# Modulation vectors summed over the partitions: column-of-ones matmuls, or a fold on VectorE ahead of four small matmuls

## The chip, the cores and the metric

One core of one Trainium2 chip runs the whole program. The metric is the device time of one execution in microseconds (us). Three runs of the kernel before took 1532.04, 1532.3 and 1536.19 us; their median is 1532.3 us. Engines are named as in the profile: PE (TensorE), DVE (VectorE), ACT (ScalarE), POOL (GpSimd) and SP, which issues the loads.

## What is computed

The reference is one step of a trunk of two layers for 384 tokens (128 of context, 256 latent) with 1024 features, all in float32. Each layer is a SwiGLU block, an attention mixer and a second SwiGLU block. Every one of these sub-layers takes a shift, a scale and a gate per feature, for two groups of tokens. These come from one linear map per layer:

```
def _adaln(cvec, w, b):
    m = jax.nn.silu(cvec) @ w + b
    return m.reshape(cvec.shape[0], N_MOD, D_MODEL)     # N_MOD = 9, D_MODEL = 1024

h = _rms_norm(x, g[0]) * (1 + m[:, :, 1]) + m[:, :, 0]
x = x + 0.5 * m[:, :, 2] * _swiglu(h, w13[0], w2[0])
```

So a layer has nine vectors m of 1024 features, each for two conditioning vectors (context and latent). The change concerns how these vectors are added up.

## The kernel before, in words

Activations lie feature-major: eight chunks of 128 features by 384 tokens. Each float32 operand of a large product is split into a high and a low part, and a product is three matmuls (`mm3`, L176 to L180): high by high (L178), high by low (L179), low by high (L180). Weights come as tiles of 1024 rows by 256 columns through a stream (`Weights`). SP loads three tiles ahead (L75), ACT makes the high half `wh` (L80) and DVE the low half `wl` (L84), again three tiles ahead of their use.

A SwiGLU block (`ffn`, `swiglu`) goes through the hidden features in three stages. Each stage first makes its chunks of gates and ups: products named proj, silu on ACT to `sg` (L611), `gf` as their product on DVE (L618), then the split of `gf` into `gh` on ACT (L628) and `gl` on DVE (L629). Then come eight products named down, which read all `gh` and `gl` of the stage, and DVE adds each to the residual `x` (L359). Products go to four PSUM buffers in turn.

The first two modulation vectors are made apart, chunk by chunk, in the setup. The other 16 are made beside the large products. A weight chunk `wm` of 128 rows by 1024 columns is loaded for each of eight k. In `tick`, the first chunk's product with the two conditioning columns is written by ACT to two accumulators `macc` of 128x1024 (L217, L218), and the other seven are added by DVE, one multiply-add for each accumulator (L221). For the first of the 16 vectors a part of that goes over ACT (L226) and POOL (L227), and DVE does one accumulator (L228). `pace` is called after each chunk of a product and decides by a rate whether a tick is issued. When the last k of a vector is done, `m_sums` is set and no tick is issued for three further calls (`mod_finish`, called after each chunk). Then `mod_sum` issues the sum over the 128 partitions. Eight matmuls at L269, four for each accumulator, have a column of ones as weights and 256 of the 1024 columns as the moving operand; each goes to its own 32 partitions of a PSUM tile `m_sum`. In the trace a float32 matmul shows as two passes, so a vector has sixteen. DVE then transposes blocks of 32x32 (L274, `m_tr`), and `mod_place` adds the bias (L288) and finishes scales (L290) and halved gates (L295). The ticks that were held back follow at once.

All engines run their instructions in the order in which the program issues them, and the order is the one written here. Setup fills `onecol` by memsets on POOL (L1331, L1333).

Of the kernel before, what the change touches and what calls it, by code (L numbers as in the profile page):

```python
# [8 lines left out]
F32 = mybir.dt.float32  # L9
# [3 lines left out]
ALU = mybir.AluOpType  # L13
AX = mybir.AxisListType

P = 128
D = 1024
# [41 lines left out]
class Weights:  # L59
    """A stream of weight tiles: loads run ahead, then each is split into two float32r parts."""  # L60
# [37 lines left out]
    def start_half(self):  # L98
        """The high parts of the next half tile."""
        if self.cur is None:  # L100
            self.load(self.ns + 1)
            self.cur = (self.raw.pop(self.ns), self.split_tiles())
            self.at = 0
        self.end = min(self.at + 4, self.units[self.ns].nk)
        self.high(*self.cur, self.at, self.end)

    def end_half(self):
        """The low parts of it."""
        k = self.k
        self.low(*self.cur, self.at, self.end, k.nc.gpsimd if self.at and k.light else k.nc.vector)  # L110
        self.at, self.end = self.end, 0
        if self.at == self.units[self.ns].nk:
            self.parts[self.ns] = self.cur[1]
            self.cur = None
            self.ns += 1
            self.load(self.ns + self.LOADED)
# [7 lines left out]
    def refill_half(self):  # L124
        """A half tile at a time, the low parts a call after the high ones."""
        if self.end:
            self.end_half()
        if self.ns < min(self.np + self.SPLIT, len(self.units)):
            self.start_half()
# [16 lines left out]
class Unit:  # L146
    """A weight tile: nk row chunks of 128 from r0, 256 columns from c0."""
# [6 lines left out]
class Kernel:  # L154
# [20 lines left out]
    def mm3(self, out, w, x, first, last):  # L175
        """out += w.T @ x over float32 operands given as (high, low) float32r parts."""  # L176
        mm = self.nc.tensor.matmul
        mm(out, w[0], x[0], start=first, stop=False)  # L178
        mm(out, w[0], x[1], start=False, stop=False)  # L179
        mm(out, w[1], x[0], start=False, stop=last)  # L180
# [5 lines left out]
    def rsqrt_cols(self, v, out):  # L186
        """out = v ** -0.5 for a few columns."""
        n = v.shape[-1]
        self.nc.gpsimd.tensor_tensor(out=out, in0=v, in1=self.neghalf[:, 0:n], op=ALU.pow)  # L189

# [11 lines left out]
    def tick(self, n=1):  # L202
        """n row chunks of the next modulation vectors: products and sums over the rows of a partition."""
        nc = self.nc
        self.m_debt += n
        while self.m_debt:
# [26 lines left out]
            if k == KC - 1:  # L233
                self.m_sums, self.m_wait = (l, i), 3

    def pace(self):
        """A chance for ticks: as many as the rate of this part has added up to."""
        self.m_credit += 1.0 if self.m_calls < 10 else 0.9 if self.m_calls < 60 else 0.72
        self.m_calls += 1
        while self.m_credit >= 1:  # L240
            self.m_credit -= 1
            self.tick(1)
# [7 lines left out]
    def mod_finish(self, n):  # L250
        """Sum over the partitions, features to partitions, bias; some work after the last tick."""
        nc = self.nc
        if self.m_sums is None:
            return
        self.m_wait -= n
        if self.m_wait > 0:
            return
        self.mod_sum()
        self.tick(0)

    def mod_sum(self):
        nc = self.nc
        l, i = self.m_sums
        self.m_sums = None
        ps = self.ps("at", "m_sum")
        for g in range(2):
            v = self.macc[g].rearrange("p (b j r) -> p j b r", b=8, j=4, r=32)
            for j in range(4):
                nc.tensor.matmul(  # L269
                    ps[32 * j:32 * j + 32, 0:256], self.onecol[:, g, :], v[:, j],  # L270
                    start=(g == 0), stop=(g == 1),
                )
        tr = self.a2("m_tr")[:, 0:256].rearrange("p (b c) -> p b c", b=8)
        nc.vector.transpose(tr.rearrange("p b c -> p (b c)"), ps[:, 0:256])  # L274
        m = self.keep.tile([P, 8, 2], F32, name=f"m_{l}_{i}", tag=f"m_{l}_{i}")
        self.m[l, i] = m
        self.mod_place(l, i, slice(0, 8), tr[:, :, 0:2])

    def mod_place(self, l, i, cs, rows):
        """m[l, i] for chunks cs: rows + bias; a scale becomes (1 + scale) * g."""  # L280
# [16 lines left out]
    def first_mod_load(self, oc):  # L297
        """The first sub-layer's scale and shift weights for one chunk of features, [P, 2, P] per row chunk."""
# [21 lines left out]
    def first_mod(self, oc, ts):  # L320
        """Scale and shift of the first sub-layer for one chunk of features: sums in four groups of rows."""
# [23 lines left out]
    def square_sum(self, oc):  # L345
        """Squares of a chunk; returns what adds them up."""
# [9 lines left out]
    def x_update(self, oc, psum, gate, nxt):  # L356
        """Residual update of one chunk; then its part of the next norm."""
# [23 lines left out]
    def pre_norm(self, l, n, oc):  # L381
        """The two parts of [x * g * (1 + scale) | shift]: the norm's factor comes after the product."""
# [23 lines left out]
    def norm_factor(self):  # L406
        """Columns of 1 / rms, a token a partition."""
# [16 lines left out]
    def norm_rows(self):  # L424
        """The factors of all tokens in every partition."""
# [9 lines left out]
    def norm_chunk(self, l, n, oc):  # L435
        """xs[oc] = the two parts of rms_norm(x) * g * (1 + scale) + shift; feature-major."""
# [31 lines left out]
        # three stages, a chunk apart  # L468
# [8 lines left out]
    def table(self, f):  # L477
        """Have the scalar engine's table for f loaded ahead of its use."""
        self.nc.scalar.activation(self.small(1, "tab", 2), self.ones, f)

    def first_project(self, l, n, f):
        """Two weight tiles against the parts of [x * a | shift]; the norm is finished on the way."""
# [49 lines left out]
    def project_pieces(self, c, res, n):  # L532
        """The same in pieces of n row chunks; the product goes to res."""
# [69 lines left out]
    def swiglu(self, g, at, gates):  # L603
        """One weight tile of gates (unless they are there), one of ups: two chunks."""
# [34 lines left out]
    def out_start(self, gs, order, tags, first=0):  # L639
        """The first two weight tiles over half of the chunks of gs, a chunk at a time; first tiles ahead of the others."""  # L640
# [33 lines left out]
    def head_rows(self, squares):  # L674
        """Sums of squares over 64 features: a row for each half of each chunk, at partitions 32j, 32j + 1."""
# [9 lines left out]
    def head_rstd(self, rs, name, scale):  # L685
        """rsqrt(mean square + eps) * scale, scale a power of two; tokens to partitions: [P, 3, chunks, 2]."""
# [15 lines left out]
    def rope(self, out, src):  # L702
        """out, src: [P, 256] latent tokens, feature-major."""
# [13 lines left out]
    def scaled_and_squares(self, psum, g, out, j):  # L717
        """out = psum * g (per feature); the squares of psum."""
# [6 lines left out]
    def first_squares(self, tile, g, out, j):  # L725
        """The same for a product that still lacks the norm's factor and the shift's part."""
# [11 lines left out]
    def finish_keys(self, ks, rk, j, kt):  # L738
        """Normalise keys, rotate the latent ones: kt = [cached | latent | own context]."""
# [14 lines left out]
    def values(self, v_tiles, c0):  # L754
        """One weight tile as the moving operand: token-major values."""
# [14 lines left out]
    def load_cache(self, name, n):  # L770
        """Cached context keys and values, token-major."""
# [14 lines left out]
    def pipeline(self, n, a, m, b, c, lag, fill, refill):  # L786
        """a, m, b and c are the stages of n steps; fill is other work for the gaps."""
# [13 lines left out]
    def even_mixer(self, l):  # L801
# [8 lines left out]
        # keys  # L810
# [6 lines left out]
        # queries; the keys' norms meanwhile  # L817
# [12 lines left out]
        # values  # L830
# [17 lines left out]
        def fill(s):  # L848
            next(conv, None)
            if s == 10:  # L850
                # context keys, token-major
# [64 lines left out]
    def even_attention(self, q, kt, vt, rq, go):  # L916
# [3 lines left out]
        def scores(i, h):  # L920
            """Scaled scores' exponentials, weighted and subtracted: the list of [P, keys] maps."""
# [159 lines left out]
    def odd_mixer(self, l):  # L1081
# [26 lines left out]
        def queries():  # L1108
            """Pieces of the other queries' products; their norms and rotations some pieces later."""
# [79 lines left out]
    def odd_attention(self, qs, rq, kt, vt, gs):  # L1189
        """Per step two query heads 4u + 2c, 4u + 2c + 1 and one tile of queries; heads 4u .. 4u + 3 share a key head."""  # L1190
# [3 lines left out]
        def scores(u, c, i):  # L1194
            # a half of the partitions for each parity of the head
# [92 lines left out]
    def setup(self):  # L1288
# [22 lines left out]
        # the first two weight tiles come in pieces, between the modulation's  # L1311
# [18 lines left out]
        self.onecol = keep.tile([P, 2, 32], F32, name="onecol")  # L1330
        nc.gpsimd.memset(self.onecol, 0.0)  # L1331
        for g in range(2):
            nc.gpsimd.memset(self.onecol[:, g, g:g + 1], 1.0)  # L1333
# [12 lines left out]
        # residual stream, feature-major; the squares' sums from the token-major rows  # L1346
# [17 lines left out]
        # the first sub-layer's modulation chunk by chunk, each with its part of the first product  # L1364
# [211 lines left out]
```

## Time and profile before

| what | value |
|---|---|
| median of three runs | 1532.3 us |
| span of the profiled execution, first to last instruction | 1533.8 us |
| its mean granted clock of PE | 0.989 |
| busy PE, DVE, ACT, POOL | 98%, 71%, 43%, 12% of the span |
| 16 sums at L269 on PE, time with at least one of them running | 17.6 us |
| 16 transposes at L274 on DVE | 7.1 us |

The profiled execution has no time of its own beside its span; the span stands 1.5 us above the median and inside the range of the three runs. A time such as 269.31 is counted from the first instruction. A row of the timeline gives start, duration, engine, line, operation, names and shapes, and in brackets how long the engine was idle before it and what ended that. Matmuls overlap, so their durations do not add up; the step from one start to the next says what one costs.

### The profile page before, as it was taken

To read this page: it belongs to the slowest core of one execution; us is meant where nothing else is said; L and a number is where in the kernel's file an instruction comes from. 1 tells how busy PE (TensorE), PEld (TensorE's weight loads), DVE (VectorE), ACT (ScalarE), POOL (GpSimd) and SP (SyncE) were. 2 spreads that over 40 slices of the span, in tenths; PEclk is the share of its full clock that TensorE was granted. 3 is DMA by queue.
4 is the path that set the end of the run, shared out by engine and by line. 5 is a ranking of instruction groups with operands and counts; after the bars stand their busy time and mean duration, and the time that the engine had idled before them with its cause. 6 is when DMAs were issued, how large, how long until landed. Compare 5 with 4: busy or idle time off the path is not lost.

```text
span 1533.8 us, 22554 instructions
## 1 busy us (share of the span) xinstructions
PE 1496.8 (98%) x8938; PEld 1419.5 (93%) x8938; DVE 1087.1 (71%) x1723; ACT 665.4 (43%) x1218; POOL 188.5 (12%) x120
## 2 busy tenths in 40 slices
PE   7989999999999999999999999999999999999998
PEld 5888999999899999999999999999965799999998
DVE  2799888868786887787779868876785386444432
ACT  3653333366555642334454333325565564232331
POOL 2450000005322100000010000000453230000000
PEclk9999999999999999999999999999997999999999
DMA  9767677642323376576536656743320034433431
GB/s 292 233 221 234 226 242 259 220 151 90 110 83 124 116 255 220 179 246 221 178 110 218 223 179 222 243 165 111 109 74 29 4 111 137 138 98 127 142 102 41
DMA packets 204555, 248.60 MB, mean 162 GB/s; under 512 B 5957, under 2 KB 186786, under 8 KB 204450
## 3 DMA queue, kind: packets, MB, share of 16 engines
q1 hardware_dynamic: 203374, 245.79, 48.6%
q8 instruction: 70, 1.15, 0.3%
q10 hardware_dynamic: 1076, 1.38, 0.3%
q14 instruction: 35, 0.29, 0.1%
HBM read 244.26 MB, written 2.36 MB: 161 GB/s over the span
## 4 chain that ended last, share of the span: by engine, by line
PE 85%; DVE 7%; ACT 3%; issue 2%; POOL 1%; DMA 1%; SPq 0%; ACTq 0%; DVEq 0%; POOLq 0%
PE proj L178 17%; PE proj L180 17%; PE proj L179 17%; PE down L179 8%; PE down L178 8%; PE down L180 8%; PE s L1202 2%; DVE wl L84 2%; PE m_sum L269 1%; PE oo L1259 1%; ACT wh L80 1%; PE aT L1246 1%; DVE acc L354 1%; DVE macc L228 1%; DVE x L359 1%
## 5 line engine op out<-in xcount | busy, mean ns | idle before, releaser
L178 PE MATMUL proj<-xh,wh 128*128 128x384 f32 (+1 forms) x1648 | 562.8, 342 | 1.1 <-ACT xh L391 1.1
L179 PE MATMUL proj<-xl,wh 128*128 128x384 f32 (+1 forms) x1648 | 556.8, 338 | 2.3 <-DVE xl L463 2.2
L180 PE MATMUL proj<-xh,wl 128*128 128x384 f32 (+1 forms) x1648 | 556.1, 337 | 0.0
L84 DVE TENSOR_TENSOR wl<-raw,wh 128x1024 fp32r<-128x1024 f32 (+1 forms) x292 | 352.6, 1246 | 131.2 <-ACT wh L80 130.6
L80 ACT ACTIVATE wh<-raw 128x1024 fp32r<-128x1024 f32 (+1 forms) x330 | 317.3, 1012 | 150.9 <-PE down L179 81.8
L178 PEld LDWEIGHTS proj<-xh,wh 128*128 128x128 f32 x1648 | 310.4, 188 | 16.2 <-issue 9.5
L179 PEld LDWEIGHTS proj<-xl,wh 128*128 128x128 f32 x1648 | 310.9, 189 | 3.6 <-DVE xl L463 3.2
L180 PEld LDWEIGHTS proj<-xh,wl 128*128 128x128 f32 x1648 | 310.4, 188 | 0.0
L178 PE MATMUL down<-gh,wh 128*128 128x384 f32 x832 | 280.8, 337 | 8.2 <-ACT gh L628 8.2
L179 PE MATMUL down<-gl,wh 128*128 128x384 f32 x832 | 279.3, 336 | 1.6 <-DVE gl L629 1.6
L180 PE MATMUL down<-gh,wl 128*128 128x384 f32 x832 | 278.6, 335 | 0.0
L221 DVE SCALAR_TENSOR_TENSOR macc<-wm,cpad,macc 128x1024 f32<-128x1024 f32 x210 | 259.1, 1278 | 0.3 <-issue 0.3
L178 PEld LDWEIGHTS down<-gh,wh 128*128 128x128 f32 x832 | 156.4, 188 | 11.6 <-ACT gh L628 8.8
L179 PEld LDWEIGHTS down<-gl,wh 128*128 128x128 f32 x832 | 156.4, 188 | 3.6 <-DVE gl L629 3.3
L180 PEld LDWEIGHTS down<-gh,wl 128*128 128x128 f32 x832 | 156.4, 188 | 0.0
L628 ACT ACTIVATE gh<-gf 128x768 fp32r<-128x768 f32 x44 | 37.3, 848 | 262.2 <-DVE gf L618 256.9
L359 DVE SCALAR_TENSOR_TENSOR x<-down,m,x 128x128 f32<-128x128 f32 x224 | 82.5, 411 | 72.9 <-PE down L180 72.9
L611 ACT ACTIVATE sg<-proj 128x384 f32<-128x384 f32 x78 | 37.8, 488 | 147.2 <-PE proj L180 147.1
L84 POOL TENSOR_TENSOR wl<-raw,wh 128x1024 fp32r<-128x1024 f32 (+1 forms) x38 | 82.7, 2189 | 134.1 <-ACT wh L80 105.4
L618 DVE TENSOR_TENSOR gf<-proj,sg 128x384 f32<-128x384 f32 x78 | 43.2, 554 | 68.4 <-PE proj L180 68.4
L189 POOL TENSOR_TENSOR nr<-nv,neghalf 128x3 f32<-128x3 f32 x6 | 5.1, 853 | 573.0 <-DVE nv L418 573.0
L629 DVE TENSOR_TENSOR gl<-gf,gh 128x768 fp32r<-128x768 f32 x44 | 42.2, 958 | 40.2 <-ACT gh L628 40.2
(212 smaller groups left out, 1168.5 us busy)
## 6 DMA issues: line engine op xcount, KB each, us to landing
raw<-in_ffn_w SPq DMA_DIRECT2D x117, 1024.0 KB, 5.3
wm<-in_w_mod SPq DMA_DIRECT2D x128, 512.0 KB, 4.1
raw<-in_ffn_w SPq DMA_DIRECT2D x16, 768.0 KB, 5.9
raw<-in_even_w_in SPq DMA_DIRECT2D x12, 1024.0 KB, 5.2
wm<-in_w_mod SPq DMA_DIRECT2D x24, 256.0 KB, 6.1
raw<-in_odd_w_in SPq DMA_DIRECT2D x6, 1024.0 KB, 4.8
raw<-in_even_w_out SPq DMA_DIRECT2D x4, 1024.0 KB, 5.0
raw<-in_odd_w_out SPq DMA_DIRECT2D x4, 1024.0 KB
```

The costliest lines, as they stand in the source:

```text
L80: self.k.nc.scalar.activation(parts[0][:, a:b], raw[:, a:b], AF.Copy)
L84: engine.tensor_tensor(out=lo[:, a:b], in0=raw[:, a:b], in1=h[:, a:b].bitcast(F32), op=ALU.subtract)
L178: mm(out, w[0], x[0], start=first, stop=False)
L179: mm(out, w[0], x[1], start=False, stop=False)
L180: mm(out, w[1], x[0], start=False, stop=last)
L221: nc.vector.scalar_tensor_tensor(out=acc, in0=t, scalar=c, in1=acc, op0=ALU.mult, op1=ALU.add)
L359: self.nc.vector.scalar_tensor_tensor(out=self.x[oc][:, a:b], in0=psum[:, a:b], scalar=gate[:, oc, g:g + 1], in1=self.x[oc][:, a:b], op0=A ...
L611: nc.scalar.activation(sg[c], out[:, 0:T], AF.Silu)
L618: nc.vector.tensor_tensor(out=gf[:, c], in0=out[:, 0:T], in1=sg[c], op=ALU.mult)
L628: nc.scalar.activation(gh[:, at:at + 2], gf, AF.Copy)
L629: nc.vector.tensor_tensor(out=gl[:, at:at + 2], in0=gf, in1=gh[:, at:at + 2].bitcast(F32), op=ALU.subtract)
L1202: nc.tensor.matmul(s[p][:, 0:n], qs[u][hs, c, i * P:(i + 1) * P], keys[p][hs, k0:k0 + n], start=True, stop=(i == 0),)
```

## The change

The sum over 128 partitions is made in two parts. Right behind the last multiply-add of a vector, `tick` calls the new `mod_fold`: for each accumulator DVE transposes 32x32 blocks of all 1024 columns into a scratch tile, and reduces each run of 32 columns to one, which adds up 32 partitions. The result `m_red` is 128 partitions by 64 values. `mod_sum`, issued where it was, then adds the four remaining groups of partitions by four matmuls of 16 columns each, with a 128x32 matrix of four stacked unit matrices as weights. The transpose behind the sum goes, and `mod_place` reads PSUM. The scratch tile shares the tag `wp` with the product of L226. In the setup three additions on POOL build the weight matrix from the unit matrix, in place of the memsets of `onecol`. Removed doc strings and comments, which the diff also has, are left out.

```diff
@@ tick
             if k == KC - 1:
                 self.m_sums, self.m_wait = (l, i), 3
+                self.mod_fold()
@@ mod_sum
         ps = self.ps("at", "m_sum")
-        for g in range(2):
-            v = self.macc[g].rearrange("p (b j r) -> p j b r", b=8, j=4, r=32)
-            for j in range(4):
-                nc.tensor.matmul(
-                    ps[32 * j:32 * j + 32, 0:256], self.onecol[:, g, :], v[:, j],
-                    start=(g == 0), stop=(g == 1),
-                )
-        tr = self.a2("m_tr")[:, 0:256].rearrange("p (b c) -> p b c", b=8)
-        nc.vector.transpose(tr.rearrange("p b c -> p (b c)"), ps[:, 0:256])
+        red = self.m_red.rearrange("p (b j) g -> p j b g", j=4)
+        for j in range(4):
+            nc.tensor.matmul(
+                ps[32 * j:32 * j + 32, 0:16], self.fold, red[:, j], start=True, stop=True,
+            )
         m = self.keep.tile([P, 8, 2], F32, name=f"m_{l}_{i}", tag=f"m_{l}_{i}")
         self.m[l, i] = m
-        self.mod_place(l, i, slice(0, 8), tr[:, :, 0:2])
+        self.mod_place(l, i, slice(0, 8), ps[:, 0:16].rearrange("p (b g) -> p b g", g=2))
+
+    def mod_fold(self):
+
+        nc = self.nc
+        self.m_red = self.work.tile([P, 32, 2], F32, tag="m_red", name="m_red", bufs=1)
+        for g in range(2):
+            tr = self.wpool.tile([P, D], F32, tag="wp", name="m_tr", bufs=1)
+            nc.vector.transpose(tr, self.macc[g])
+            nc.vector.tensor_reduce(
+                out=self.m_red[:, :, g], in_=tr.rearrange("p (b r) -> p b r", r=32), axis=AX.X, op=ALU.add
+            )
@@ setup
-        self.onecol = keep.tile([P, 2, 32], F32, name="onecol")
-        nc.gpsimd.memset(self.onecol, 0.0)
-        for g in range(2):
-            nc.gpsimd.memset(self.onecol[:, g, g:g + 1], 1.0)
+
+        self.fold = keep.tile([P, 32], F32, name="fold")
+        nc.gpsimd.tensor_tensor(out=self.fold, in0=self.ident[:, 0:32], in1=self.ident[:, 32:64], op=ALU.add)
+        for q in (2, 3):
+            nc.gpsimd.tensor_tensor(
+                out=self.fold, in0=self.fold, in1=self.ident[:, 32 * q:32 * q + 32], op=ALU.add
+            )
```

## Rows read from the trace of the kernel before

**Rows 1.** The page's busy time of each engine (time, share of the span, instructions) and, from the chain of work that ended last, its shares of the span by line.

```profile
PE 1496.8 (98%) x8938; PEld 1419.5 (93%) x8938; DVE 1087.1 (71%) x1723; ACT 665.4 (43%) x1218; POOL 188.5 (12%) x120
...
PE proj L178 17%; PE proj L180 17%; PE proj L179 17%; PE down L179 8%; PE down L178 8%; PE down L180 8%; PE s L1202 2%; DVE wl L84 2%; PE m_sum L269 1%; PE oo L1259 1%; ACT wh L80 1%; PE aT L1246 1%; DVE acc L354 1%; DVE macc L228 1%; DVE x L359 1%
```

**Rows 2.** The timeline of the matmuls around the sum of vector 5, and below it the weight loads of that sum.

```profile
269.05 0.34 PE L180 MATMUL proj<-xh,wl 128*128 128x384 f32 x1
269.31 1.07 PE L269 MATMUL m_sum<-macc,onecol 128*32 128x256 f32 x16
270.31 0.44 PE L178 MATMUL proj<-xh,wh 128*128 128x384 f32 x1
...
269.31 0.59 PEld L269 LDWEIGHTS m_sum<-macc,onecol 128*32 128x32 f32 x16 [0.25 <-issue]
```

**Rows 3.** The timeline of the matmuls around the sums of squares of a norm (six passes of one column, weights of 128 columns).

```profile
503.99 0.83 PE L411 MATMUL ss<-ones,acc 128*128 128x1 f32 x6 [0.36 <-DVE acc L354]
504.69 0.42 PE L178 MATMUL proj<-xh,wh 128*128 128x386 f32 x1
```

**Rows 4.** Groups of instructions by line and shape: busy us, mean ns of one, idle time before them.

```profile
L221 DVE SCALAR_TENSOR_TENSOR macc<-wm,cpad,macc 128x1024 f32<-128x1024 f32 x210 | 259.1, 1278 | 0.3 <-issue 0.3
...
L269 PE MATMUL m_sum<-macc,onecol 128*32 128x256 f32 x256 | 17.6, 394 | 0.0
...
L274 DVE STREAM_TRANSPOSE m_tr<-m_sum 128x256 f32<-128x256 f32 x16 | 7.1, 447 | 7.9 <-PE m_sum L269 7.9
...
L955 DVE TENSOR_REDUCE mx<-s 128x1 f32<-128x384 f32 x16 | 8.1, 548 | 1.2 <-PE s L937 1.2
...
L949 DVE TENSOR_REDUCE mx<-s 128x4 f32<-128x512 f32 x2 | 1.3, 680 | 0.0
```

**Rows 5.** The timeline of POOL in the setup, behind the memsets.

```profile
13.12 0.86 POOL L189 TENSOR_TENSOR nr<-nv,neghalf 128x3 f32<-128x3 f32 x1 [11.71 <-DVE nv L418]
```

**Rows 6.** The timeline around the end of vector 1: DVE, ACT and the product that waits.

```profile
111.94 3.36 DVE L228 SCALAR_TENSOR_TENSOR macc<-wm,cpad,macc 128x1024 f32<-128x1024 f32 x1
...
115.22 1.01 DVE L618 TENSOR_TENSOR gf<-proj,sg 128x384 f32<-128x384 f32 x2
...
116.26 0.84 ACT L628 ACTIVATE gh<-gf 128x768 fp32r<-128x768 f32 x1 [5.28 <-DVE gf L618]
...
117.16 0.69 PE L178 MATMUL down<-gh,wh 128*128 128x384 f32 x1 [7.56 <-ACT gh L628]
```

**Rows 7.** The timeline of DVE and of PE around the sum of vector 4.

```profile
225.95 2.47 DVE L221 SCALAR_TENSOR_TENSOR macc<-wm,cpad,macc 128x1024 f32<-128x1024 f32 x2
...
230.38 1.07 PE L269 MATMUL m_sum<-macc,onecol 128*32 128x256 f32 x16
```

**Rows 8.** From vector 4 to vector 6: what DVE waited for from 231.9 to 300.58 (us in total, times, longest), then its timeline at the end of vector 6, then PE's.

```profile
DVE wl L84 <- ACT wh L80: 2.5, 3, 2.1
DVE gf L618 <- PE proj L180: 2.4, 2, 1.7
...
300.58 0.55 DVE L618 TENSOR_TENSOR gf<-proj,sg 128x384 f32<-128x384 f32 x1
302.05 0.96 DVE L629 TENSOR_TENSOR gl<-gf,gh 128x768 fp32r<-128x768 f32 x1 [0.92 <-ACT gh L628]
...
303.07 0.43 PE L179 MATMUL down<-gl,wh 128*128 128x384 f32 x1
```

**Rows 9.** The timeline at the ends of vectors 7, 9, 14, 3 and 11, in this order: the last multiply-adds on DVE, and what stands behind the fold there.

```profile
560.36 2.47 DVE L221 SCALAR_TENSOR_TENSOR macc<-wm,cpad,macc 128x1024 f32<-128x1024 f32 x2
...
565.65 1.07 PE L269 MATMUL m_sum<-macc,onecol 128*32 128x256 f32 x16
...
650.78 2.47 DVE L221 SCALAR_TENSOR_TENSOR macc<-wm,cpad,macc 128x1024 f32<-128x1024 f32 x2
...
657.42 0.96 DVE L629 TENSOR_TENSOR gl<-gf,gh 128x768 fp32r<-128x768 f32 x1 [0.92 <-ACT gh L628]
...
658.44 0.45 PE L179 MATMUL down<-gl,wh 128*128 128x384 f32 x1 [0.26 <-DVE gl L629]
...
934.98 2.47 DVE L221 SCALAR_TENSOR_TENSOR macc<-wm,cpad,macc 128x1024 f32<-128x1024 f32 x2
...
190.58 2.47 DVE L221 SCALAR_TENSOR_TENSOR macc<-wm,cpad,macc 128x1024 f32<-128x1024 f32 x2
195.66 1.83 DVE L84 TENSOR_TENSOR wl<-raw,wh 128x1024 fp32r<-128x1024 f32 x2 [2.61 <-ACT wh L80]
...
739.49 2.47 DVE L221 SCALAR_TENSOR_TENSOR macc<-wm,cpad,macc 128x1024 f32<-128x1024 f32 x2
...
746.66 1.07 PE L269 MATMUL m_sum<-macc,onecol 128*32 128x256 f32 x16
```

**Rows 10.** The timeline of DVE at the end of vector 2.

```profile
148.68 2.47 DVE L221 SCALAR_TENSOR_TENSOR macc<-wm,cpad,macc 128x1024 f32<-128x1024 f32 x2
...
160.91 2.36 DVE L84 TENSOR_TENSOR wl<-raw,wh 128x1024 fp32r<-128x1024 f32 x2 [5.40 <-ACT wh L80]
```

**Rows 11.** A product after a short wait, in the timeline of PE, and two stretches by engine: stretch, us, busy time (instructions) of PE, PEld, DVE, ACT and POOL, granted clock of PE, DMA share, GB/s.

```profile
206.44 0.44 PE L178 MATMUL down<-gh,wh 128*128 128x384 f32 x1 [0.61 <-ACT gh L628]
...
117.10:119.00 1.90, 1.53 (x4) 1.14 (x5) 1.86 (x2) 1.90 (x3) 0.00 (x0) 0.50 0.47 190
...
206.40:210.00 3.60, 3.01 (x15) 2.75 (x16) 3.58 (x6) 1.46 (x2) 0.00 (x0) 1.00 0.41 137
```

## The prediction, as it was put on record before the changed kernel ran

> **What bounds the kernel now.** I read the page's busy times first: TensorE works 1496.8 us of a span of 1533.8 us, VectorE (DVE) 1087.1 us [rows 1]. The chain of waits says the same by line: the big products at L178 to L180 carry it, and the sums at L269 stand in it with 1% of the span. So an instruction taken from TensorE pays by what it takes of TensorE's queue, and one added on DVE costs nothing until something that TensorE waits for comes late. The average of DVE hides just that, so I then went through the timeline of DVE around each of the 16 modulation vectors (numbered 1 to 16 in order of their sums).
>
> **What is removed on TensorE.** Around the sum of vector 5, the last L180 starts at 269.05, the sixteen passes of m_sum at 269.31, the next product at 270.31 [rows 2]. The passes hold the queue for 1.00 us; the 0.26 us ahead of them belongs to the change of kind and stays. Their weight loads take 0.59 us, 0.037 us apiece. The new sum has half the passes (8 loads) and 16 columns instead of 256 each, so I set it at 8 x 0.037 = 0.30 plus 0.1 for the last pass: 0.4 us, a gain of **0.6 us a vector**. Bounds: nothing left would be a gain of 1.0; the nearest row of short float32 matmuls, six of one column with 128-column weights, holds the queue for 0.70 us from 503.99 to 504.69 [rows 3], which for eight is 0.93, a gain of 0.07. I take 0.6 since the weights here are 32 columns wide, as in [rows 2].
>
> A pass of m_sum lasts 394 ns in the mean, yet sixteen end within 1.07 us [rows 2, 4], so four of them run side by side. The Trainium skill (TensorE: Matmul & The Clock Gate, Part 3: Packing small matmuls, Measured speedup vs the span model) gives such a pack one matmul's duration and 4 ns for each further tile. With the 0.39 us of the old pass as an upper estimate, two packs would be 0.80 us, the gain 0.2 us a vector, and the sum below about 6 us worse; the order of the trace agrees, the duration of a 16-column pass is in no row.
>
> **What is added on DVE: the fold.** Per vector two transposes and two reduces of 128x1024, issued right behind the last multiply-add of the vector. The transpose of 128x256 takes 0.447 us; reduces take 0.548 us at 384 columns and 0.680 at 512 [rows 4], so 1.03 ns a column. Then a transpose is 0.447 + 768 x 1.03 ns = 1.24, a reduce 0.680 + 512 x 1.03 ns = 1.21, two of each 4.90, and with a little for each waiting on the one before, **5.0 us**. Bounds: 4 passes at the 1.2 us step of the multiply-adds (2.47 for two) are 4.8; below that, half the rate or 2.6, only if a source in SBUF (all rows are from PSUM) is read twice as fast; above, 7.2, if the transpose runs at half its rate. The 0.45 us transpose of m_tr goes. I take 5.0.
>
> **Parts that cost nothing.** The three POOL adds that build the fold matrix stand where memsets stood: POOL then waits 11.71 us until 13.12 [rows 5], and without that cover they would be below a microsecond. No DMA is added; weight loads that SP issues behind a delayed wl go 5 us later, three tiles ahead of use. ACT's first multiply of the next vector waits for the fold's reads instead of TensorE's. The bias add reads 16 columns from PSUM instead of SBUF.
>
> **Where the fold lands.** DVE runs in program order, so all behind it is 5.0 us later until an idle wait takes it up; m_sum itself now waits for it. Vector by vector:
> - Vector 1: the last multiply-add ends at 115.2, then come gf (115.22), gh on ACT (116.26) and the product at 117.16, which has already waited 7.56 us for this chain [rows 6]. The whole fold goes into it: **+5.0**.
> - Vector 4: the last multiply-adds end at 228.4, m_sum starts at 230.38 [rows 7]. The fold ends at 233.4, TensorE stands still: **+3.0**.
> - Vector 6: the last multiply-adds end at 300.6, and gf, gh, gl follow; the product that needs gl starts with no slack (303.07, 0.43 us long where its like take 0.34) [rows 8]. That is 5.0, and DVE arrives late: folds 4 and 5 add 10.0, less 0.9 for two m_tr, less 2.4 by which TensorE itself was moved (3.0 - 0.6), plus 0.6 gained at vector 5, less 4.9 of idle waits for wh and proj: at most 2.4 left, of which I count 1.7, as smaller waits take up some more. **+6.7**.
> - Vector 7: last multiply-add done 562.8, fold 567.9, m_sum due 565.65 [rows 9]: **+2.2**.
> - Vectors 9 and 14: the last ends at 653.2 (937.4), the fold at 658.2; two gf (0.5 each), gh (0.85), then gl at 660.1 instead of 657.42, with TensorE already waiting for it at 658.44: **+2.6 each**.
> - Vector 3: fold until 198.1, wl due at 195.66; most of the 2.4 us comes back before the end of the stage: **+0.3**. Vector 11: fold until 747.0, m_sum due 746.66: **+0.4**.
> - The other eight: as in vector 2, where the fold would end at 156.1 and DVE idles 5.40 us ahead of 160.91 [rows 10], idle waits take it up; what is late next (x, wl) has four PSUM buffers or three weight tiles of slack.
>
> The stalls sum to 5.0 + 3.0 + 6.7 + 2.2 + 5.2 + 0.3 + 0.4 = 22.8 us. After the stall of 7.5 us at vector 1 the granted clock was 0.50 from 117.1 to 119.0 (the 1.2 GHz level); after the wait of 0.61 us ahead of 206.44 it was 1.00 [rows 11]. Vector 6's new stall is near the first: I add 1.5 us (some 4 us at half rate, in part while waiting anyway). Gains: 15 x 0.6 = 9.0, vector 3's being lost in the wait behind it. **Net +15.3 us.** The profiled execution has a span of 1533.8, within 0.1% of the median of 1532.3; against the median: **1547.6 us**.
>
> **Rivals.**
> - *Cheap fold* (the other side). At a price p, vectors 1 and 6 still cost p each, vector 4 p - 2.0, vectors 7, 9 and 14 p - 2.8 each, the rest nothing. It decides below p = 3.3, where these stalls reach 9.6, the gain of 16 sums. With p = 2.6: 5.8 - 9.6 = -3.8, so 1528.5. For it: no row has a transpose or a wide reduce out of SBUF. Against: the multiply-adds out of SBUF go at 1.2 ns a column. Chance 0.10. The Trainium skill speaks against it too: VectorE: DVE Perf Modes (The perf-mode tier table) gives a reduce only the single rate, and Vector Engine (DVE) Microarchitecture Reference (3.8) one element per cycle and lane for the transpose; the 0.447 us row agrees, for a source in PSUM.
> - *Cover*: the delays are taken up as in vector 2, and TensorE keeps 9.6 us: 1522.7. For it: eight vectors behave so and DVE idles 29% of the span. Against: [rows 6 to 9], where too little that is idle lies between. Chance 0.07.
> - *Clock*: the stalls of 2 to 3 us at vectors 4, 7, 9 and 14 drop the clock as well, 2 us each: 1555.6. Against: the 0.6 us wait did not; for: the 7.5 us one did. Chance 0.12.
> - *No gain on TensorE*: the sum with its eight passes stays near 0.93 us [rows 3]: 15.3 + 8 gives 1555.6. Chance 0.06.
> - *Dear fold*, 7.2 us: 2.2 more at the eight late vectors, and some of the covered ones late: about +36, 1568. Chance 0.08.
>
> **How the numbers follow.** The forecast has 0.57, with 1540 to 1557 as its own range (price 4.6 to 5.5, gain 0.3 to 0.9). 0.3% is 4.6 us, about what a measurement of this kernel can tell from no change. Faster by more: all of cover and half of cheap fold, 0.12. Within it: the other half of cheap fold, and 0.05 of the forecast's low tail, 0.10. Slower: 0.78. The range reaches from the cheap fold to past the two rivals at 1556: 1528 to 1560; cover, the lower half of cheap fold and the dear fold stay outside, 0.20.
>
> **What the changed profile would show.** m_sum with 8 passes and about 0.4 us between the products around it; fold instructions of some 1.2 us each, 64 in all; TensorE idle ahead of m_sum at vectors 4 and 7, ended by the reduce on DVE; ahead of the down products at vectors 1 and 6 longer by 5 us or more, at 9 and 14 by 2.6. I am wrong if the fold's instructions are half as long, or if DVE's order is not the program's, so that gf goes ahead of the fold.

## The result, and the profile after

The changed kernel takes 1552.5 us in the median of four runs (1547.6 to 1553.5), the kernel before 1532.2 (1530.3 to 1536.2): a ratio of 1.0126, 95% interval 1.0112 to 1.0140. It is slower. The profiled execution has a span of 1550.6 us (before 1533.8) and a mean granted clock of 0.981 (before 0.989).

The page of the changed kernel first: busy time by engine, and the chain by line (to be laid beside [rows 1]).

```profile
PE 1491.8 (96%) x8810; PEld 1422.7 (92%) x8810; DVE 1154.3 (74%) x1771; ACT 664.6 (43%) x1218; POOL 188.7 (12%) x120
...
PE proj L178 14%; PE proj L180 14%; PE proj L179 14%; PE down L179 8%; PE down L178 8%; PE down L180 8%; DVE macc L221 4%; DVE wl L84 4%; PE s L1210 2%; ACT wh L80 2%; DVE m_tr L282 1%; DVE m_red L283 1%; PE oo L1267 1%; DVE acc L362 1%; PE aT L1254 1%
```

TensorE is busy 5 us less, its slower products included, and DVE 67 us more. The chain shows what that buys: m_sum is no longer among its lines, DVE's low halves (L84) have gone from 2% to 4%, and more of DVE's multiply-adds (L221) and the fold (L282, L283) have come into it. The groups of instructions, as in [rows 4]:

```profile
L282 DVE STREAM_TRANSPOSE m_tr<-macc 128x1024 f32<-128x1024 f32 x32 | 39.8, 1243 | 0.5
L283 DVE TENSOR_REDUCE m_red<-m_tr 128x32 f32<-128x1024 f32 x32 | 39.0, 1220 | 1.1
...
L269 PE MATMUL m_sum<-m_red,fold 128*32 128x16 f32 x128 | 4.2, 197 | 5.1 <-DVE m_red L283 5.1
```

Then the sum of vector 5, as in [rows 2], and the places where TensorE now waits, as in [rows 6 to 9]: vectors 1, 3, 4, 6, 7 and 9 in the timeline of PE, and the whole execution in the list of waits.

```profile
277.50 0.34 PE L180 MATMUL proj<-xh,wl 128*128 128x384 f32 x1
277.76 0.26 PE L269 MATMUL m_sum<-m_red,fold 128*32 128x16 f32 x8
277.95 0.44 PE L178 MATMUL proj<-xh,wh 128*128 128x384 f32 x1
...
121.90 0.69 PE L178 MATMUL down<-gh,wh 128*128 128x384 f32 x1 [13.93 <-ACT gh L636]
...
209.94 0.45 PE L178 MATMUL down<-gh,wh 128*128 128x384 f32 x1 [1.59 <-ACT gh L636]
...
238.08 0.26 PE L269 MATMUL m_sum<-m_red,fold 128*32 128x16 f32 x8 [2.58 <-DVE m_red L283]
...
315.16 0.69 PE L178 MATMUL down<-gh,wh 128*128 128x384 f32 x1 [4.47 <-ACT gh L636]
...
582.61 0.26 PE L269 MATMUL m_sum<-m_red,fold 128*32 128x16 f32 x8 [2.29 <-DVE m_red L283]
...
676.93 0.44 PE L178 MATMUL down<-gh,wh 128*128 128x384 f32 x1 [2.05 <-ACT gh L636]
```

```profile
PE down L178 <- ACT gh L636: 24.1, 5, 13.9
PE m_sum L269 <- DVE m_red L283: 5.1, 3, 2.6
```

The sum between two products now holds the queue for 0.18 us in place of 1.00. Before, the waits for gh came to 8.2 us in two places; now they are 24.1 us in five, and three waits of the sum for the fold (vectors 4, 7 and 11, 5.1 us) come on top. DVE at vector 6 shows how such a wait arises: the fold stands between the multiply-adds and the gf on which gh, and so the down product, depends.

```profile
306.35 2.48 DVE L221 SCALAR_TENSOR_TENSOR macc<-wm,cpad,macc 128x1024 f32<-128x1024 f32 x2
308.74 1.24 DVE L282 STREAM_TRANSPOSE m_tr<-macc 128x1024 f32<-128x1024 f32 x1
310.02 1.22 DVE L283 TENSOR_REDUCE m_red<-m_tr 128x32 f32<-128x1024 f32 x1
311.27 1.25 DVE L282 STREAM_TRANSPOSE m_tr<-macc 128x1024 f32<-128x1024 f32 x1
312.55 1.22 DVE L283 TENSOR_REDUCE m_red<-m_tr 128x32 f32<-128x1024 f32 x1
313.69 0.55 DVE L626 TENSOR_TENSOR gf<-proj,sg 128x384 f32<-128x384 f32 x1
315.14 0.96 DVE L637 TENSOR_TENSOR gl<-gf,gh 128x768 fp32r<-128x768 f32 x1 [0.91 <-ACT gh L636]
```

What is not a wait is seen only in the step from one product to the next. Behind vector 4 it goes from 0.17 to 0.32 us while the engine is never idle (PE's timeline; then four stretches: start and end, us, busy time of each engine, granted clock, DMA share, GB/s):

```profile
238.90 0.36 PE L178 MATMUL proj<-xh,wh 128*128 128x384 f32 x1
239.07 0.50 PE L179 MATMUL proj<-xl,wh 128*128 128x384 f32 x1
239.37 0.52 PE L180 MATMUL proj<-xh,wl 128*128 128x384 f32 x1
239.69 0.52 PE L178 MATMUL proj<-xh,wh 128*128 128x384 f32 x1
...
239.37:242.25 2.88, 2.88 (x10) 2.88 (x10) 2.88 (x6) 0.48 (x1) 0.00 (x0) 0.50 0.07 13
...
212.32:215.20 2.88, 2.88 (x11) 2.88 (x10) 2.88 (x5) 0.00 (x0) 0.00 (x0) 0.50 0.40 122
...
584.35:587.23 2.88, 2.88 (x11) 2.88 (x10) 2.85 (x6) 0.00 (x0) 0.00 (x0) 0.50 0.40 108
587.30:590.20 2.90, 2.90 (x18) 2.90 (x17) 1.22 (x2) 0.77 (x2) 0.00 (x0) 1.00 1.08 388
```

That is the lower level, 1.2 GHz (0.50), where [rows 11] had it once, behind vector 1. Such stretches of ten or eleven products lie behind vectors 3, 4, 7 and 9, one of sixteen behind 6 and one of nine behind 14; behind vector 1, where the kernel before has one too, it costs 0.63 us more than there. Behind vector 6 the first product is slow already (0.69 us); behind 3, 4, 7 and 9 the slow steps begin 1 to 2.6 us after TensorE took up work again.

**The balance.** Laying the starts of the same products of both traces beside each other splits the shift:

| part | us |
|---|---|
| waits, vectors 1, 3, 4, 6, 7, 9, 11, 14: 4.7 + 1.0 + 2.7 + 5.8 + 2.4 + 2.6 + 0.3 + 2.6 | +22.1 |
| slow steps behind them: vectors 1, 3, 4, 6, 7, 9, 14: 0.63 + 1.46 + 1.57 + 1.90 + 1.55 + 1.58 + 1.5 | +10.2 |
| sixteen sums: 1.2 at vector 1, 15 x 0.82 | -13.5 |
| sum (the shift measured at 1105 us of the kernel before is 19.0) | +18.8 |
| behind 1105, where no modulation sum stands | -2.2 |
| the two spans, 1550.6 - 1533.8 | +16.8 |

What is given back behind 1105 us is not explained by the change: between 1160 and 1200 us the granted clock is 0.79 before and 0.91 after, in a stretch without a modulation sum. Both kernels wait 1.90 us for DVE in the odd attention, and behind that wait the clock is 0.50 for 17 us in the trace before and for 7 us in the trace after (a row of PE's timeline and a stretch of the kernel before, then a stretch of the changed kernel):

```profile
1171.10 0.91 PE L1202 MATMUL s<-okt,oq 64*128 64x384 f32 x2 [1.90 <-DVE orq_v L696]
...
1172.50:1189.30 16.80, 16.74 (x74) 9.60 (x73) 6.45 (x28) 8.05 (x29) 5.80 (x5) 0.50 0.14 48
...
1191.50:1198.10 6.60, 5.91 (x28) 3.62 (x28) 2.81 (x14) 4.54 (x14) 4.30 (x3) 0.50 0.49 159
```

That gives back 4.3 us; 2.1 us were lost just ahead of it, behind a wait of 1.81 us at 1132.56 (0.50 from 1133.5 to 1136.7), where the kernel before waited 1.20 us and kept 1.00. Executions of one kernel differ by as much (the nine-fold kernel below took 1524.0 us at a mean granted clock of 0.994 and 1529.9 at 0.988), so what two single traces differ by behind 1105 us is not to be put down to an edit.

### The profile page after: what moved, and what is told of

It reads as the page before. It is cut to its first block, busy times and chain, and to the rows that moved or that the text cites. A ratio compares the mean times of both kernels' runs of the same rounds, so it can differ in the third digit from the quotient of the medians.

```text
span 1550.6 us, 22333 instructions
## 1 busy us (share of the span) xinstructions
PE 1491.8 (96%) x8810; PEld 1422.7 (92%) x8810; DVE 1154.3 (74%) x1771; ACT 664.6 (43%) x1218; POOL 188.7 (12%) x120
## 4 chain that ended last, share of the span: by engine, by line
PE 73%; DVE 16%; ACT 3%; issue 3%; POOL 1%; DMA 1%; SPq 0%; ACTq 0%; DVEq 0%; POOLq 0%
PE proj L178 14%; PE proj L180 14%; PE proj L179 14%; PE down L179 8%; PE down L178 8%; PE down L180 8%; DVE macc L221 4%; DVE wl L84 4%; PE s L1210 2%; ACT wh L80 2%; DVE m_tr L282 1%; DVE m_red L283 1%; PE oo L1267 1%; DVE acc L362 1%; PE aT L1254 1%
## 5 line engine op out<-in xcount | busy, mean ns | idle before, releaser
L84 DVE TENSOR_TENSOR wl<-raw,wh 128x1024 fp32r<-128x1024 f32 (+1 forms) x292 | 352.6, 1247 | 102.6 <-ACT wh L80 102.3
L178 PE MATMUL down<-gh,wh 128*128 128x384 f32 x832 | 284.5, 342 | 24.1 <-ACT gh L636 24.1
L179 PE MATMUL down<-gl,wh 128*128 128x384 f32 x832 | 282.5, 340 | 2.5 <-DVE gl L637 2.5
L221 DVE SCALAR_TENSOR_TENSOR macc<-wm,cpad,macc 128x1024 f32<-128x1024 f32 x210 | 259.2, 1279 | 0.0
L84 POOL TENSOR_TENSOR wl<-raw,wh 128x1024 fp32r<-128x1024 f32 (+1 forms) x38 | 82.4, 2179 | 135.0 <-ACT wh L80 113.3
```

What stands on the lines that cost most here:

```text
L84: engine.tensor_tensor(out=lo[:, a:b], in0=raw[:, a:b], in1=h[:, a:b].bitcast(F32), op=ALU.subtract)
L221: nc.vector.scalar_tensor_tensor(out=acc, in0=t, scalar=c, in1=acc, op0=ALU.mult, op1=ALU.add)
```

## The experiments

The theory: a fold costs what TensorE waits for something behind it on DVE, by its place, plus slow steps after the wait; a covered fold costs nothing.

**The fold alone, and the small sums alone.** The kernel before with the fold added (into a result that nothing reads) and its old sums kept; and the changed kernel without the fold, its matmuls reading 64 columns of `macc`, so that the partial sum over 32 partitions is left out.

```diff
@@ the fold alone, against the kernel before
                 self.m_sums, self.m_wait = (l, i), 3
+                self.mod_fold()
...
@@ the small sums alone, against the changed kernel
-                self.mod_fold()
...
-        red = self.m_red.rearrange("p (b j) g -> p j b g", j=4)
+        red = self.macc[0][:, 0:64].rearrange("p (b j g) -> p j b g", j=4, g=2)
```

> The kernel before with the fold's 64 instructions added on VectorE at the end of each vector, and nothing done with their result; the sums stay the old ones on TensorE. Position theory (the fold costs where something that TensorE waits for stands right behind it, and the stalls then lower the granted clock): the stalls at vectors 1, 3, 6, 9 and 14 come as in the changed kernel (about 4.7 + 1.0 + 6 to 7 + 2.6 + 2.6 us), those at the sums of vectors 4 and 7 do not come, since these sums no longer wait for the fold, and 1.5 to 1.9 us of half clock follow at each of vectors 3, 6, 9, 14: 1555 to 1560 us, 23 to 28 us over the kernel before. Rival, that the loss comes from the new sums' wait for the fold: about 1535 us.

> The changed kernel without the fold: the four matmuls of 16 columns read the first 64 columns of the first accumulator, so the sum over partitions is left out of the computation. This is TensorE's gain alone. By the step between the products around the sum in the changed kernel (0.18 us against 1.00 us) it is 16 x 0.82 = 13 us, so 1519 us; by the 0.6 us of the prediction 1522.6 us. If the sums had not been on the path, 1532 us.

Measured beside 1532.8 of the kernel before: the fold alone 1560.7 us, ratio 1.0182 (1.0167 to 1.0197); the small sums alone 1519.2, ratio 0.9918 (0.9899 to 0.9936). The first lies 0.7 us over its expected range, as the slow steps expected at vector 3 did not come and more was lost at vector 6; the second is where 0.82 us a sum put it. So the fold costs 27.8 us and the sums give 13.6: TensorE gains less than DVE's lateness takes. The difference, 14.2, is 6 us short of the 20 measured for both, since the parts meet: here m_sum does not wait for the fold, so the sums of vectors 4 and 7 have no wait and no slow steps behind them, and the lateness is handed on: behind vector 7 the products lose 1.9 us at 592.69, and the product of vector 6 waits 7.91 us instead of 4.47 (PE's timeline of the fold-only kernel), with products at 0.50 behind it (319.0 to 322.8).

```profile
317.80 0.69 PE L178 MATMUL down<-gh,wh 128*128 128x384 f32 x1 [7.91 <-ACT gh L639]
```

**The fold later.** It is issued two calls later, the sum five calls behind the last multiply-add instead of three, and the ticks, the multiply-adds of the next vector, are held all that time. So the fold and the ticks are moved together.

```diff
-                self.m_sums, self.m_wait = (l, i), 3
-                self.mod_fold()
+                self.m_sums, self.m_wait, self.m_red = (l, i), 5, None
@@ mod_finish
         self.m_wait -= n
+        if self.m_wait <= 3 and self.m_red is None:
+            self.mod_fold()
...
```

> The changed kernel with the same 64 fold instructions, issued two calls (two chunks of a product) later, and the sum two calls later with them, so that in vectors 3, 6, 9 and 14 the fold stands behind the gl that TensorE waits for, and in vectors 4 and 7 the sum no longer meets an unfinished fold. Only vector 1, whose gate is needed at once, keeps a wait of about 5 us. Position theory: 13 us gained, some 6 us lost at vector 1, at most 2 us elsewhere: 1524 to 1528 us. Rival, that VectorE's 72 us of added work are the cost wherever they stand: about 1550 us.

Measured 1543.0 us, ratio 1.0069 (1.0052 to 1.0085): between the two, so the forecast missed. The waits at vectors 9 and 14 almost go, as expected, but new ones come. DVE's timeline and TensorE's waits in this kernel show why:

```profile
212.19 4.86 DVE L221 SCALAR_TENSOR_TENSOR macc<-wm,cpad,macc 128x1024 f32<-128x1024 f32 x4
218.63 2.48 DVE L221 SCALAR_TENSOR_TENSOR macc<-wm,cpad,macc 128x1024 f32<-128x1024 f32 x2 [1.58 <-DMA wm<-in_w_mod]
...
249.38 4.86 DVE L221 SCALAR_TENSOR_TENSOR macc<-wm,cpad,macc 128x1024 f32<-128x1024 f32 x4
255.94 4.87 DVE L221 SCALAR_TENSOR_TENSOR macc<-wm,cpad,macc 128x1024 f32<-128x1024 f32 x4 [1.70 <-DMA wm<-in_w_mod]
```

```profile
PE down L178 <- ACT gh L639: 11.1, 3, 7.9
PE m_sum L272 <- DVE m_red L286: 5.8, 2, 5.3
...
PE proj L178 <- DVE gf L629: 2.5, 1, 2.5
...
PE proj L178 <- DVE x L370: 1.8, 1, 1.8
PE down L178 <- DVE x L370: 1.3, 1, 1.3
```

The ticks that were held back two calls longer come in bursts of four multiply-adds and then wait for their own load; gf and x stand behind them, and with them the PSUM buffers that the next products need. A move that clears one chain filled the next.

**Filling the wait.** Fifteen unused products of 384 columns stand ahead of the sums of vectors 4 and 7, where TensorE was idle for 2.6 and 2.3 us.

```diff
+        for _ in range(15 if (l, i) in ((0, 5), (0, 8)) else 0):
+            nc.tensor.matmul(ps[:, 128:512], self.xs[0][0][:, 0:P], self.xs[1][0], start=True, stop=True)
```

> The changed kernel with 15 products of 384 columns, whose result is not used, issued ahead of the sums of vectors 4 and 7, where TensorE waits about 2.5 us for the fold. They take 15 x 0.174 = 2.6 us, the length of the wait. If the idle time there is what lowers the granted clock behind it (1.44 us lost at vector 4, 1.46 us at vector 7), the 10 slow steps behind each sum go and the kernel is about 2.5 us faster, 1550 us. If the clock falls for another reason, it stays at 1552 us or is a little slower, and the slow steps remain.

Measured 1548.7 us, ratio 1.0102 (1.0087 to 1.0117), 3.8 us below the changed kernel. In the place where the clock had been 0.50 in the changed kernel:

```profile
235.09 2.81 PE L268 MATMUL m_sum<-xh 128*128 128x384 f32 x15
237.83 0.26 PE L271 MATMUL m_sum<-m_red,fold 128*32 128x16 f32 x8
...
239.37:242.25 2.88, 2.88 (x18) 2.88 (x17) 2.88 (x6) 0.23 (x1) 0.00 (x0) 1.00 0.12 20
584.00:590.00 6.00, 6.00 (x36) 6.00 (x35) 5.05 (x9) 2.12 (x3) 0.00 (x0) 1.00 0.80 273
```

The sum starts as late as before (237.83 against 238.08), so what the fold makes late is all there; the slow steps are gone at both places and stay behind vectors 3, 6, 9 and 14. That separates the two terms: at these places the idle time costs twice, once as itself and once as slow products, whose going moves the products ahead by 1.55 us at vector 4 and 1.30 at vector 7.

The 3.8 us are not the sum of these two. The product of vector 6 waits for DVE, and as TensorE now comes to it earlier, it waits longer (4.47 us in the changed kernel):

```profile
314.40 0.69 PE L178 MATMUL down<-gh,wh 128*128 128x384 f32 x1 [5.52 <-ACT gh L638]
```

That gives back 1.05 us, and a longer stretch at 0.50 at vector 9 (675.7 to 682.3, before the fill 679.4 to 682.8) gives back 1.04. From vector 4 to 1105 us only 0.4 us is left, and 3.3 of the 4.0 us between the two spans arise behind it, where the clock differs without an edit. So the forecast of 1550 us was met in part by luck; what shows the cause is the clock in the two places, not the time.

**Vector 1 without a fold.** Vector 1 is summed by eight matmuls of 256 columns with ones as weights, and one transpose, here of 512 columns since each accumulator keeps its own 256; all other vectors as in the change.

```diff
-                self.mod_fold()
+                if (l, i) != (0, 2):
+                    self.mod_fold()
...
```

> The changed kernel, but vector 1 is summed the old way, without a fold; the other fifteen vectors as in the change. Theory: its fold stood wholly in the wait ahead of the first down product (4.7 us) and added about 0.6 us of slow steps; the old sum costs about 0.8 us more on TensorE. The product behind gh starts near 117 us again, and the time is 4 to 5 us below the changed kernel's: about 1548 us; all later stalls stay. Rival (the delay at vector 1 is in part taken up or is handed on as lateness of DVE): the gain is below 2 us, 1550 to 1552, as the later vectors then stall by more.

Measured 1547.0 us, ratio 1.0096 (1.0083 to 1.0109), against a kernel before of 1531.6 in that series; the ratio puts it 4.6 us below the changed kernel (0.0030 x 1532). The longest wait for gh falls from 13.93 to 7.7 us, and all later waits stay (1.59, 2.58, 4.45, 2.31, 2.05 and 2.05 us at vectors 3, 4, 6, 7, 9 and 14). Lateness of DVE at vector 1 is not handed on.

**A fold placed by the pair.** Vector 1 as above; a fold that would come just ahead of an up product goes behind the gl and wl of that pair; ticks are held two calls, and the sum comes five (four) calls behind the fold.

```diff
-            if self.m_sums is not None:
+            if self.m_sums is not None and (self.m_red is None or self.m_wait > self.m_hold):
                 return
...
+                self.m_sums, self.m_wait, self.m_hold, self.m_red = (l, i), 5, 3, None
+                if (l, i) == (0, 2):
+                    self.m_wait = 3
+                elif self.m_ok:
+                    self.mod_fold()
@@ swiglu
+            self.m_ok = c == 0
...
                 self.split_g(gf, g, at)
                 self.w.done()
+                self.m_ok = True
...
```

> Vector 1 is summed the old way without a fold (eight matmuls of 256 columns and one transpose). For the other fifteen the fold is issued at once, except where the vector ends just ahead of an up product: then it is issued behind the gl and wl of that pair, so that gf, gh and gl are not behind it. The ticks come back about two calls behind the fold, ahead of the sum, which is issued five calls behind the fold (four after a deferral), so that the sum does not wait for the fold and the multiply-adds are not held in bursts. Position theory (the fold costs only where TensorE waits for something behind it on DVE, and the clock falls only after such waits): the stalls at vectors 1, 4, 6, 7, 9 and 14 go, and their slow steps with them; what is left is the time with the sums free of DVE, 1519, plus 0.8 for vector 1's old sum and a few us for vectors that still meet a tight chain: 1520 to 1526 us, below both kernels. Rival (the fold's work itself costs, wherever it stands, since DVE is late on the whole): 1535 or more, with new waits for x, gf or wl in place of the old ones.

Measured 1532.8 us, ratio 1.0004 (0.9995 to 1.0014): no difference from the kernel before, 7 us over the expected range, so this forecast missed too. Both readings hold a part. The waits at 4, 9 and 14 are gone, but beside the kernel with the small sums alone the shift of products grows by 1.6 us at vector 1, 2.3 at vector 3, 5.6 at vector 6 and 2.4 at vector 7, and by 1.5 in all behind it: too many for 'a few us'. At vector 6 the fold itself now stands behind the split (309.38); what is late there is DVE's work handed on. From fold 5 (272.55 to 277.58) to the gf at 304.69 DVE is idle only in one wait of 0.9 us for gh (ahead of 291.26):

```profile
302.30 2.47 DVE L221 SCALAR_TENSOR_TENSOR macc<-wm,cpad,macc 128x1024 f32<-128x1024 f32 x2
304.69 0.55 DVE L655 TENSOR_TENSOR gf<-proj,sg 128x384 f32<-128x384 f32 x1
306.15 0.96 DVE L667 TENSOR_TENSOR gl<-gf,gh 128x768 fp32r<-128x768 f32 x1 [0.91 <-ACT gh L666]
...
309.38 1.24 DVE L310 STREAM_TRANSPOSE m_tr<-macc 128x1024 f32<-128x1024 f32 x1
```

So place decides, but place includes what DVE still has to make good from the folds before. How much of the lateness comes from the folds and how much from the moved multiply-adds, no run separates.

**Nine folds, and the other seven.** The vectors at which TensorE stood still are summed the old way and the other nine fold as in the change; and the reverse.

```diff
@@ nine folds
+OLD = (1, 3, 4, 6, 7, 9, 14)
@@ seven folds
+OLD = (2, 5, 8, 10, 11, 12, 13, 15, 16)
@@ both
...
-                self.mod_fold()
+                if self.folded():
+                    self.mod_fold()
...
+    def folded(self):
+        return self.m_done // KC not in OLD
```

> The changed kernel, but the seven vectors at which TensorE stood still for the fold (1, 3, 4, 6, 7, 9 and 14) are summed the old way, without a fold; the nine others fold as in the change, at the same place. Position theory: these nine folds are free, so no stall and no slow step is added to those of the kernel before, and each of the nine sums gives 0.82 us: 1532.2 - 7.4 + 0.3 (vector 11) = 1525, between 1523 and 1528, faster than both kernels. Rival (the folds make DVE late on the whole, and the lateness comes out at the next tight place, whoever folds there): vector 6 behind fold 5, 9 behind 8 and 14 behind 13 still stall by some us each, and the time is 1531 or more.

> The complement: only vectors 1, 3, 4, 6, 7, 9 and 14 fold, the nine others are summed the old way. Position theory: all stalls of the changed kernel and their slow steps stay, only the gain of nine sums goes: 1552.5 + 7.4 = 1560, less up to 1 us at vector 6, whose stall the prediction put down in part to fold 5: 1558 to 1561. Rival (stalls come from the work of all sixteen folds together): with seven of them the stalls fall to half, and the time is near 1546 to 1550.

Nine folds: 1525.6 us, ratio 0.9962 (0.9949 to 0.9976), faster than both kernels, inside its range and 0.6 us above the 1525 expected. Seven folds: 1556.8, ratio 1.0164 (1.0151 to 1.0177), slower than all sixteen. In the nine-fold kernel no stretch of products between the setup and the odd attention goes at half clock but the one behind vector 1 that the kernel before has too. Vector 4 (old sum) and vector 5 (fold) in its timeline begin within 0.1 us of [rows 7] and [rows 2]:

```profile
230.47 1.07 PE L276 MATMUL m_sum<-macc,ones 128*32 128x256 f32 x16
231.47 0.44 PE L180 MATMUL proj<-xh,wh 128*128 128x384 f32 x1
...
269.41 0.26 PE L286 MATMUL m_sum<-m_red,fold 128*32 128x16 f32 x8
269.60 0.44 PE L180 MATMUL proj<-xh,wh 128*128 128x384 f32 x1
```

At each of the nine folded vectors the products move ahead by 0.81 or 0.82 us (vector 11 gives back 0.29). One fold is not quite free: behind fold 5 the products at vector 6 lose 0.5 us, with a wait of 0.35 us for gl at 302.87, so the rival holds there, for a small part. In the seven-fold kernel vector 6 costs 0.7 us less without fold 5 (its wait for gh is 3.94 us instead of 4.47), and the waits at vectors 3, 4, 7, 9 and 14 differ by at most 0.2 us from those of the change. Its median is 1.3 us under the expected range; with the kernel before at 1530.9 in that series instead of the 1532.2 used, the ratio puts it at 1557.3.

## Why the prediction was right, and where it was off

The forecast was 1547.6 us, slower, net +15.3; measured +20.3 in the medians, +16.8 in the profiled spans. By its steps:

- **Fold price** (5.0 us from rows of other widths): 1.243 us a transpose and 1.220 a reduce, four of them 4.93. Right. A reduce of 1024 columns is at 1.19 ns a column, a multiply-add at 1.25. The Trainium skill (VectorE: DVE Perf Modes, The perf-mode tier table) gives a reduce no faster mode than the single rate, and the trace agrees. The rivals *cheap fold* and *dear fold* fall with it.
- **Stalls** (22.8 us): 22.1 measured, each at its place. Two were put differently: vector 3 cost 1.0, not 0.3, and vector 6 cost 5.8, not 6.7. That fold 5 bears on vector 6 the two kernels with part of the folds confirm, at 0.7 us (seven folds) and 0.5 us (nine), where the prediction had 1.7 for folds 4 and 5 together. *Cover* holds for eight vectors and not for the rest, as the prediction read it; the nine-fold kernel shows it as a time (it has vector 11 besides, which gives back 0.3).
- **Gain of a sum** (0.6 us): 0.82. The step that failed is "8 x 0.037 for the loads plus 0.1 for the last pass": the eight loads and passes together hold the queue 0.18 us, less than the 0.30 set for the loads alone. The six passes of [rows 3], the bound from the other side, had 128-column weights and did not bear on it. *No gain on TensorE* falls. Nor do four of the old passes run side by side, as the prediction read it: sixteen of 0.39 us in 1.07 us are about six at a time, so a group of four does not wait for the end of the one before. The estimate by the pack rule of the Trainium skill (TensorE: Matmul & The Clock Gate, Part 3: Packing small matmuls) was 0.80 us for the new sum; with the 0.20 us that a pass of 16 columns lasts by its row it would be 0.42, still more than twice the 0.18 measured, and for the four groups of the old sum it gives 1.61 against 1.00. So pack behind pack the rule, as it was used, counts too much here.
- **Clock** (1.5 us, at vector 6 alone): 10.2 us, at seven vectors. This is the term that was mis-sized, and the mechanism is the one of the rival *clock*: waits of 1.6 to 2.6 us were followed by products at 0.50, 1.5 us each. The prediction weighed two rows, 0.61 us of waiting with the clock at 1.00 behind it and 7.5 us with 0.50, and put 2 to 3 us with the short one. The trace of the kernel before had rows between, which were not read: 1.02 us (ahead of 508.07) and 1.20 us (ahead of 1113.00) with 1.00 behind them, 1.37 us in the setup (ahead of 63.78) and the 1.90 us ahead of 1171.10 with 0.50. The filled wait shows, at vectors 4 and 7, that the idle time lowers the clock. Its length alone does not decide: the fold-only kernel has the same setup and a wait of 1.35 us at the same place, and kept 1.00 (a stretch of the kernel before, then one of the fold-only kernel):

```profile
66.50:69.80 3.30, 3.30 (x12) 3.12 (x12) 3.30 (x4) 1.19 (x4) 2.37 (x1) 0.50 0.56 180
...
67.00:70.30 3.30, 3.30 (x20) 3.13 (x19) 3.30 (x4) 1.18 (x4) 2.38 (x1) 1.00 0.52 167
```

The two mis-sized terms have opposite signs: 4.5 us more gain against 8.7 us more clock. With 0.7 us less of stalls that makes 3.5 of the 4.9 us by which the forecast was low; the rest lies within what single executions of one kernel differ by. The direction comes from the right cause, the stalls; that the number stayed inside the forecast's own range owes something to luck, as the two errors cancel by half.

What stays open: why, behind the same wait of 1.90 us in the odd attention, the clock stays at 0.50 for 17 us in some traces (the kernel before, nine folds) and for 3 to 7 us in others, and what beside the length of a wait decides whether the clock falls.

## What to carry to other kernels

Work moved from a full engine to one that idles 29% is priced vector by vector, from the order of instructions behind it: nine of sixteen folds were all but free (0.8 us of waits) and seven cost more than all sixteen sums saved. Keep the cheaper form only where the chain behind it has slack, and keep the old form elsewhere; deferring the work for every vector alike, with the ticks held back, made new waits. And price each new wait of TensorE with the slow products that may follow it, here 1.5 us on top of 1.6 to 2.6; the trace at hand may already show what waits of that length did elsewhere.

## What the runs showed of the hardware

The granted clock fell to 0.50 after waits such as the 1.59 us ahead of 209.94, not at once but 2.1 us into the work that followed (1.0 us behind the 2.58 us ahead of 238.08), and stayed there for ten products (2.88 us) in both places, with TensorE busy throughout; where the wait ahead of the sums of vectors 4 and 7 was filled with unused products it stayed at 1.00. It stayed at 1.00 behind waits of 1.04 us (ahead of 205.92, sums alone) and 1.11 us (ahead of 213.28, fold alone), and behind one of 1.84 us too (ahead of 1102.37, sums alone). Eight float32 passes of 16 columns, in four groups of 32 PSUM partitions, hold TensorE's queue for 0.18 us with their weight loads, sixteen of 256 columns 1.00 us. A DVE transpose of 32x32 blocks over 1024 float32 columns costs about what a multiply-add of that width costs (1.243 against 1.279 us), and the reduce behind it, which completes a sum over 32 partitions, the same again (1.220).
